# One more pair of output tiles by seven products, rope tables in slots, and an instruction order planned with other TensorE costs, in a hybrid MLA and sparse-attention block

## The chip, the cores and the metric

The kernel runs on one core of a Trainium2 chip. A time is the device time of one execution in microseconds (us). The program drives five engines, each with its own queue of instructions: TensorE (PE, with its weight loads shown apart as PEld), VectorE (DVE), ScalarE (ACT), GpSimd (POOL) and SyncE (SP), which issues most of the loads and stores. All values are 32-bit floats.

## What is computed

One pre-norm layer on x, 512 tokens by 1024 channels, with two token mixers that read one combined projection of the normalised input. Cut to what matters:

```python
h = rmsnorm(x, norm_g)
(q_lat, c_kv, k_rope, z_a, q_b, k_b, v_b, z_b,
 q_idx, k_idx, w_idx, gate_a, gate_b) = split(h @ w_in)
q  = rmsnorm(q_lat) @ w_uq          # 8 heads, 64 plain and 32 rotary channels
kv = rmsnorm(c_kv) @ w_ukv          # 8 heads, 64 key and 64 value channels
y_a = chunk_causal_attention(q, kv, rope(k_rope)) * silu(z_a)        # branch a, MLA
score = sum_h w_idx * relu(q_idx . k_idx)     # masked by chunks of 64
idx = top_k(score, 128)                       # per query
y_b = attention(q_b, k_b[idx], v_b[idx], t5_bias) * silu(z_b)        # branch b, DSA
merged = sigmoid(gate_a) * (y_a @ w_o_a) + sigmoid(gate_b) * (y_b @ w_o_b)
out = rmsnorm(x + merged @ w_out, final_g)
```

The gathered attention of branch b is computed as dense attention with a mask of the selected keys.

## The kernel before

**Tiles and products.** Work lies in tiles of 128 partitions by 512 columns. On-chip memory is a pool of 73 such slots (`SB`), four buffers for raw weights of 128 by 1024 (`RAW`), some fixed tiles, and eight PSUM banks. A product of full precision is made of three products of rounded parts: each operand is split into a high part (a cast, on ACT, L381) and a low part (the value less the high part, on DVE, L416, or on POOL, L418), and `mm3` multiplies high by high, high by low and low by high (L494). `split_w` and `split_t` make the parts of a weight, and `act` and `tt` record an operation on ACT, DVE or POOL. L513 is the transposes (`turn`), L523 the DMAs on SP.

A *single* tile (`proj`, a lower-case name in the queue) is 128 output channels by 512 tokens: 8 steps over the channels of h, three matmuls of 512 columns each, 24 in all, and two splits of weights. A *pair* (`proj2`, two upper-case names) makes two such tiles at once, split in halves of tokens and channels, by seven products instead of eight (`seven`): 84 matmuls of 256 columns in place of 48 of 512. In return it needs sums of raw weights (`prep`, in the raw tiles and in `wsum` slots), sums of the input's halves (`input_sums`, `hs`, made once), seven splits instead of four, and it is put together in two `pair` slots by copies on ACT and two 256-wide adds on DVE.

**Stages.** First the latents of both branches from x (`early_x`, `early_w`, `early_mm`; 0 to some 60 us); then the projections, in the order of a list `QUEUE` (ga and gb the gates, za and zb the SiLU inputs, ma and va the MLA queries, keys and values, sb and VB the DSA queries, keys and values, pe the rotary part), with other work between them: the index scores (L961), the top-k rounds on DVE (16 rounds of MAX8, L986, and MATCH_REPLACE8, L987, for each of three masks), eight MLA heads and eight DSA heads. In the profile an MLA head is three matmuls of logits (L1909 to L1911), maxima on DVE (TENSOR_REDUCE, L1893), exponentials on ACT, transposes, high and low parts of the transposed probabilities (`ph`, `last`) and the product with the values (`vv`). A DSA head has its softmax in one custom operation on DVE (L1992). Then come the products with w_o, the seven products with w_out, and the final norm with the stores of the result.

**What sets the order.** `Flow` is a planner in the kernel's Python: each operation is a `Step` with a cost and the engines that can take it; threads with priorities yield steps, ask for slots (`Get`) or wait for conditions (`Until`), and at each turn the step that could start first by the model's times is emitted. So the place of every instruction in all five queues, and whether DVE or POOL does a subtraction, follows from `QUEUE`, from the priorities and caps below it (`PSCORE` for the index scores, `PHEAD` for the heads, `PHCAP`, `WCAP`, `TCAP`, `PCAP` for how many slots of a kind may be in use), and from the costs: `stream(n)` is that of a matmul of n columns, `turn` that of a transpose.

**Loads on the path.** MLA head logits read q and k tiles that SP's DMAs fill (`s_op`), the last of them with the shared rotary key (`kpeh`, `kpel`, the high and low parts). The same queue of SP takes raw weights (`raw<-w_ga` and so on; `fetcher`, 512 KB for a single tile) and spills of the a-branch's gates to memory (`bias_scratch<-s_sig`, 256 KB).

Of the kernel before, what the change touches and what calls it, by code (L numbers as in the profile page):

```python
# [20 lines left out]
P = 128  # L21
# [18 lines left out]
NSLOT = 73  # L40
# [260 lines left out]
def tile_block(ctx: ExitStack, tc: tile.TileContext, a: dict, out: bass.AP, bias_dram: bass.AP):  # L301
# [13 lines left out]
    def fixed(name, shape, dt=F32):  # L315
        return Buf(const.tile(shape, dt, name=name), name)
# [9 lines left out]
    SB = Pool_([Buf(None, f"s{i}") for i in range(NSLOT)], fresh)  # L326
# [158 lines left out]
    def stream(n):  # L485
        return max(0.0134 + n / 2400, 0.109)
# [20 lines left out]
    def turn(parts):  # L507


        def emit():  # L510
            for d, s in parts:
                product_to(d, True)
                nc.tensor.transpose(d.ap, s.ap, ident.tile)  # L513

        return pe(0.0875 * len(parts), [d for d, _ in parts], [s for _, s in parts] + [ident.all], emit, len(parts))
# [58 lines left out]
    ropec = fixed("ropec", [P, S])  # L574
    ropes = fixed("ropes", [P, S])
# [5 lines left out]
    junk = fixed("junk", [P, S])  # L581
# [5 lines left out]
    rbs = fixed("rbs", [P, P], F32R)  # L587
# [38 lines left out]
    def setup_pool():  # L626
# [6 lines left out]
        yield from pool_dma(ropec.all, a["ropec"])  # L633
        yield from pool_dma(ropes.all, a["ropes"])
# [91 lines left out]
    rbc = []  # L726
# [131 lines left out]

    def rope(dst, src, rows):
# [4 lines left out]
        yield tt(dst, src, ropec[rows], ALU.mult)  # L864
        yield tt(sw.all.f[rows], sw.all.f[rows], ropes[rows], ALU.mult, BOTH)
# [211 lines left out]
    def bias_table():  # L1077
        yield is_done("loads", BIAS_AT)

        yield from pool_dma(rb.all, a["rel_bias"])  # L1080
        yield memset("POOL", rbs.all.f, 0.0)
# [20 lines left out]
        put(*oh, toep, toep2)  # L1102
# [1343 lines left out]
NORM_ABIAS = -0.4  # L2446
# [133 lines left out]
```

## Time and profile before

| | |
|---|---|
| median of 3 runs | 428.67 us (427.9 to 429.76) |
| the profiled execution | 429.5 us, its span 427.7 us |
| mean granted TensorE clock in it | 0.991 |
| PE, DVE, ACT, POOL busy | 97%, 88%, 69%, 24% of the span |
| moved by DMA | 65.91 MB, mean 154 GB/s |

The span runs from the first to the last instruction in the trace; the 1.8 us between span and time lie around it. Busy times of neighbours that overlap in an engine's pipeline are counted once in the windows of the trace, while a group's mean is that of a single instruction from its own start to its own end, so counts times means come out above the busy time of a window.

### The profile page before, as it was taken

Reading aid. Unit: us, or ns where it says so; the run is one execution under the profiler, and the core shown is the slowest. Engines: PE = TensorE matmul, PEld = TensorE weight load, DVE = VectorE, ACT = ScalarE, POOL = GpSimd, SP = SyncE. Lnnn points to the kernel's source line nnn. Section 1 sums busy time; section 2 is a strip of 40 time slices with the busy share of each in tenths; the row PEclk is TensorE's granted clock in tenths of the full one; section 3 lists DMA queues with packets and bytes.
Section 4 is the critical chain, followed back from the end, with each engine's and each line's share of the span. In section 5 each row is a group of like instructions: output and inputs, shape, how many; then the busy total and the mean of one; then the engine's idle time right before and its main releaser. Section 6 shows DMA issues by size and latency. Waiting matters only on the chain.

```text
span 427.7 us, 7455 instructions
## 1 busy us (share of the span) xinstructions
PE 415.5 (97%) x2451; PEld 369.4 (86%) x2451; DVE 375.5 (88%) x801; ACT 293.5 (69%) x669; POOL 101.6 (24%) x126
## 2 busy tenths in 40 slices
PE   8999999899999999999999999999999999999993
PEld 6989888698888888888999998999988888888882
DVE  4869779589999999998969959999989876999994
ACT  5876986368685847648857698898689643348534
POOL 1032856122854442811112002111000000000212
PEclk9999999989999999999999999999999999999998
DMA  8982645605645361350243644522583884458105
GB/s 260 396 311 69 163 116 154 179 2 129 193 123 159 99 203 49 94 166 25 100 149 111 183 140 103 157 64 85 164 267 125 263 280 171 172 163 329 50 1 197
DMA packets 30279, 65.91 MB, mean 154 GB/s; under 512 B 4648, under 2 KB 5688, under 8 KB 30240
## 3 DMA queue, kind: packets, MB, share of 16 engines
q1 hardware_dynamic: 29120, 63.82, 47.2%
q0 software_dynamic: 832, 1.22, 1.0%
q8 instruction: 19, 0.31, 0.3%
q10 hardware_dynamic: 288, 0.39, 0.3%
q14 instruction: 20, 0.16, 0.1%
HBM read 50.49 MB, written 4.21 MB: 128 GB/s over the span
## 4 chain that ended last, share of the span: by engine, by line
PE 63%; DVE 17%; DMA 9%; ACT 5%; issue 3%; SPq 2%; POOL 0%; POOLq 0%; ACTq 0%; DVEq 0%
PE ps L494 54%; PE ps L513 5%; DVE s_w L416 2%; DVE s_wo L416 2%; DMA raw<-w_o 2%; DVE s_mg L416 2%; ACT s_w L381 2%; SPq L523 2%; DMA s_op<-kpel 1%; DMA raw<-w_ql 1%; DMA s_x<-xT 1%; DMA s_xn<-x 1%; DVE s_pair L416 1%; DVE s_rg L416 1%; PE ps L1910 1%
## 5 line engine op out<-in xcount | busy, mean ns | idle before, releaser
L494 PE MATMUL ps<-s_h,s_w 128*128 128x512 f32 (+1 forms) x684 | 149.5, 357 | 1.1 <-ACT s_pair L381 0.6
L494 PEld LDWEIGHTS ps<-s_h,s_w 128*128 128x128 f32 x684 | 110.3, 189 | 15.6 <-ACT s_pair L381 1.5
L381 ACT CAST s_w<-raw 128x512 fp32r<-128x512 f32 (+3 forms) x132 | 76.0, 595 | 22.0 <-DMA raw<-w_o 12.7
L416 DVE TENSOR_TENSOR s_w<-raw,s_w 128x512 fp32r<-128x512 f32 (+2 forms) x95 | 62.1, 674 | 3.9 <-ACT s_w L381 3.5
L418 POOL TENSOR_TENSOR s_w<-raw,s_w 128x512 fp32r<-128x512 f32 (+2 forms) x37 | 44.5, 1207 | 61.7 <-ACT s_w L381 30.7
L494 PE MATMUL ps<-s_hs,s_w 128*128 128x256 f32 x336 | 46.7, 285 | 0.0
L494 PE MATMUL ps<-s_ys,s_w 128*128 128x512 f32 x192 | 43.9, 389 | 0.0
L494 PEld LDWEIGHTS ps<-s_hs,s_w 128*128 128x128 f32 x336 | 42.8, 191 | 0.4 <-DVE s_w L416 0.2
L494 PEld LDWEIGHTS ps<-s_ys,s_w 128*128 128x128 f32 x192 | 36.0, 188 | 7.4
L494 PE MATMUL ps<-s_w,s_xg 128*128 128x328 f32 (+1 forms) x192 | 33.1, 325 | 0.3 <-ACT s_rbc L381 0.2
L494 PE MATMUL ps<-s_wo,s_mg 128*128 128x512 f32 (+1 forms) x156 | 33.0, 373 | 0.0
L494 PEld LDWEIGHTS ps<-s_w,s_xg 128*128 128x128 f32 x192 | 31.3, 188 | 1.2 <-ACT s_rbc L381 0.5
L494 PEld LDWEIGHTS ps<-s_wo,s_mg 128*128 128x128 f32 x156 | 27.6, 188 | 5.2
L390 ACT ACTIVATE s_p<-ps,sm 128x128 f32<-128x128 f32 (+3 forms) x32 | 16.9, 528 | 17.7 <-DVE sm L1893 17.5
L390 ACT ACTIVATE s_p<-s_p,sm 128x512 f32<-128x512 f32 (+3 forms) x52 | 28.7, 571 | 0.1
L986 DVE MAX8 sm<-mask 128x8 f32<-128x256 f32 (+2 forms) x48 | 25.6, 550 | 0.6 <-POOL mask L568 0.2
L987 DVE MATCH_REPLACE8 mask<-sm,mask 128x256 f32<-128x256 f32 (+2 forms) x48 | 26.0, 543 | 0.1
L513 PE MATMUL ps<-ident,s_p 128*128 128x128 f32 x160 | 23.1, 274 | 0.0
L494 PE MATMUL ps<-s_lat,s_w 128*128 128x512 f32 x78 | 20.7, 397 | 0.0
L513 PEld LDWEIGHTS ps<-ident,s_p 128*128 128x128 f32 x160 | 18.5, 140 | 2.1
L1992 DVE CUSTOM_DVE_ANT_0 s_p<-ps,mask 128x128 f32<-128x128 f32 (+3 forms) x32 | 15.1, 488 | 5.7 <-PE ps L494 5.3
L418 POOL TENSOR_TENSOR s_pair<-s_pair 128x256 f32<-128x256 f32 x1 | 0.7, 743 | 81.2 <-issue 81.2
(213 smaller groups left out, 800.2 us busy)
## 6 DMA issues: line engine op xcount, KB each, us to landing
raw<-w_out SPq DMA_DIRECT2D x18, 512.0 KB, 4.6
s_op<-s_op SPq DMA_DIRECT2D x36, 128.0 KB, 2.7
raw<-w_ga SPq DMA_DIRECT2D x8, 512.0 KB, 4.3
raw<-w_gb SPq DMA_DIRECT2D x8, 512.0 KB, 4.3
raw<-w_o SPq DMA_DIRECT2D x16, 256.0 KB, 3.1
s_x<-xT SPq DMA_DIRECT2D x8, 256.0 KB, 4.0
s_xn<-x SPq DMA_DIRECT2D x8, 256.0 KB, 5.7
raw<-w_za SPq DMA_DIRECT2D x4, 512.0 KB, 4.8
```

Of the source, the lines that this page charges most:

```text
L381: nc.scalar.copy(dst.ap, src.ap)
L390: nc.scalar.activation(dst.ap, src.ap, func, **kw)
L416: opts.append(("DVE", 0.07 + 0.00104 * x.n + few(x), lambda: nc.vector.tensor_tensor(dst.ap, x.ap, y.ap, op=op)))
L418: opts.append(("POOL", 0.15 + 0.0021 * x.n, lambda: nc.gpsimd.tensor_tensor(dst.ap, x.ap, y.ap, op=op)))
L494: nc.tensor.matmul(ps.ap, l.ap, r.ap, start=start and i == 0, stop=stop and i == len(pairs) - 1, skip_group_check=more)
L513: nc.tensor.transpose(d.ap, s.ap, ident.tile)
L523: return Step([("SP", n / 360000.0, lambda: nc.sync.dma_start(d, s))], bufs(dst), bufs(src))
L986: yield Step([("DVE", t, lambda: nc.vector.max(m8.tile, work.ap))], [m8], [mask[i]])
L987: yield Step([("DVE", t - 0.009, lambda: nc.vector.match_replace(work.ap, m8.tile, work.ap, MARK))], [mask[i]], [m8])
L1910: nc.tensor.matmul(o, q0[0:96], k1[0:96], start=False, stop=False)
L1992: step = Step([("DVE", 0.1 + 0.00104 * n, lambda: nc.vector.tensor_tensor_reduce(p.ap, ps.tile[:, :n], mask[i].tile, op0=ALU.add, op1=ALU. ...
```

## The change

1. **Costs of the order's model.** `stream(n)` from 0.0134 + n/2400 to 0.0148 + n/2400 (0.0133 + n/2400 at 256 columns), a transpose in `turn` from 0.0875 to 0.109 us.
2. **Slots.** The rope tables move from fixed tiles into slots that come free after their three users; `rbs` (the bias table's weights) and `rbc` (the row of norms) are given back after use; `junk` becomes bfloat16; 78 slots instead of 73. Raw tiles of at most 512 columns (sixteen of w_o, two of w_va) go to slots of a class `ro`, at most four at once (`ROCAP`), instead of `RAW`.
3. **Queue.** zb0, ga6, ga7 and zb3 were single and ZB1, ZB2 a pair; now GA6, GA7 are a pair, ZB0, ZB1 another and ZB2, ZB3 a third, and VB stands ahead of GA6.
4. **Priorities and caps**, among them the index scores from 10 to 3 (a lower number goes first among threads that could start at the same time), the heads from 4 to 8.

```diff
-NSLOT = 73
+NSLOT = 78
...
-        return max(0.0134 + n / 2400, 0.109)
+        return max(0.0148 + n / 2400, 0.109) - 0.0015 * (n == 256)
...
-        return pe(0.0875 * len(parts), [d for d, _ in parts], [s for _, s in parts] + [ident.all], emit, len(parts))
+        return pe(0.109 * len(parts), [d for d, _ in parts], [s for _, s in parts] + [ident.all], emit, len(parts))
...
-    ropec = fixed("ropec", [P, S])
-    ropes = fixed("ropes", [P, S])
...
-    junk = fixed("junk", [P, S])
+    junk = fixed("junk", [P, S], BF16)
...
-    rbs = fixed("rbs", [P, P], F32R)
...
-        yield from pool_dma(ropec.all, a["ropec"])
-        yield from pool_dma(ropes.all, a["ropes"])
+        for name in ("ropec", "ropes"):
+            t = yield slot("rope")
+            yield from pool_dma(t.all.f, a[name])
+            turns.append(t)
...
+    def rbc_done():
+        rbc_users[0] -= 1
+        if not rbc_users[0]:
+            put(rbc[0])
...
+        rbs = yield slot("oh")
         yield from pool_dma(rb.all, a["rel_bias"])
-        yield memset("POOL", rbs.all.f, 0.0)
+        yield memset("POOL", rbs[:, :P].f, 0.0)
...
-            raw = yield Get(RAW)
+            raw = (yield slot("ro", ROCAP)) if sum(job.widths) <= S and ROCAP else (yield Get(RAW))
...
-NORM_ABIAS = -0.4
+NORM_ABIAS = 0.0
...
-PHCAP = 5
-WCAP = 12
-TCAP = 5
+PHCAP = 7
+WCAP = 10
+TCAP = 7
...
-PSCORE = 10.0
+PSCORE = 3.0
 PFILL = 12.0
-PHEAD = 4.0
-OUT_AT = (2, 3, 5, 10, 10, 10, 14)
+PHEAD = 8.0
+OUT_AT = (2, 3, 5, 9, 10, 11, 13)
 ORDER = [0,1,2,3]
-QUEUE = 'ga0 ga1 pe ma0 ga2 za0 va1 va0 ma1 ga3 za1 ma2 ga4 ga5 ma3 za2 za3 sb0 zb0 ga6 ga7 VB SB1 GB0 GB1 SB2 ZB1 ZB2 GB2 GB3 SB3 GB4 GB5 zb3 gb6 ou ou gb7 ou'
-LATE = 0.4
+QUEUE = 'ga0 ga1 pe ma0 ga2 za0 va1 va0 ma1 ga3 za1 ma2 ga4 ga5 ma3 za2 za3 sb0 VB GA6 GA7 SB1 GB0 GB1 SB2 ZB0 ZB1 GB2 GB3 SB3 GB4 GB5 ZB2 ZB3 gb6 ou ou gb7 ou'
+LATE = 0.75
...
-SPARE = {'w': 3, 'wo': 6, 'sig': 3}
+SPARE = {'w': 2, 'wo': 6, 'sig': 3}
 XOUT = 0
-PSUMS = 8.0
-PCAP = 11
+PSUMS = 5.0
+PCAP = 14
 BIAS_AT = ('a', 1)
 NHELD = 3
-SUMS_AT = ('a', 6)
+ROCAP = 4
+SUMS_AT = ('a', 5)
```

Counted in the order, matmuls of `s_h` with `s_w` of 512 columns go from 432 to 336, those of 256 columns (with `s_h` or `s_hs`) from 588 to 756; DVE has 783 instructions instead of 752, POOL 119 instead of 131, ACT 601 instead of 585, SP 246 instead of 245.

**SP around the first loads of the rotary key.** `s_op` are the key tiles of the first two MLA heads, `raw` the weight buffers, `bias_scratch` the spill. Before:

```order
L523 DMA raw_68<-w_uqkv 128x640
L523 DMA s_op_984<-kpeh 36x512
L523 DMA raw_69<-w_ga 128x1024
L523 DMA bias_scratch<-s_sig_1053 128x512
L523 DMA s_op_986<-kpel 32x512
L523 DMA s_op_1024<-kpeh 36x512
L523 DMA s_op_1026<-kpel 32x512
```

And after the change:

```order
L523 DMA s_op_982<-kpeh 36x512
L523 DMA bias_scratch<-s_sig_1058 128x512
L523 DMA s_op_984<-kpel 32x512
L523 DMA s_op_1025<-kpeh 36x512
L523 DMA s_op_1027<-kpel 32x512
L523 DMA raw_67<-w_ga 128x1024
L523 DMA raw_68<-w_ga 128x1024
```

The load of w_ga has moved from ahead of the first `kpel` to behind both; the spill stays ahead of it.

**DVE around the first maximum of MLA.** `mask` holds the scores of one block of queries, `sm` small results, `s_z` a SiLU tile. Before:

```order
L428 SCALAR_TENSOR_TENSOR mask_112<-ps_99,widx,mask_112 128x512
L428 SCALAR_TENSOR_TENSOR mask_110<-ps_99,widx,mask_110 128x256
L986 MAX sm_83<-mask_110 128x8
L987 MATCH_REPLACE mask_110<-sm_83,mask_110 128x256
L986 MAX sm_84<-mask_110 128x8
L987 MATCH_REPLACE mask_110<-sm_84,mask_110 128x256
L986 MAX sm_85<-mask_110 128x8
L428 SCALAR_TENSOR_TENSOR s_z_1108<-s_z_1108,ps_95 128x512
L1893 TENSOR_REDUCE sm_86<-ps_98 128x1
```

And after the change:

```order
L999 MATCH_REPLACE mask_108<-sm_82,mask_108 128x256
L998 MAX sm_86<-mask_109 128x8
L998 MAX sm_85<-mask_108 128x8
L999 MATCH_REPLACE mask_109<-sm_86,mask_109 128x384
L428 SCALAR_TENSOR_TENSOR mask_110<-ps_98,widx,mask_110 128x512
L999 MATCH_REPLACE mask_108<-sm_85,mask_108 128x256
L998 MAX sm_87<-mask_109 128x8
L998 MAX sm_88<-mask_108 128x8
L1906 TENSOR_REDUCE sm_89<-ps_99 128x1
```

Two masks' top-k rounds have begun ahead of the first maximum where there was one; that maximum is the 133rd instruction of DVE instead of the 126th.

**DVE up to the low part of DSA head 1's transposed probabilities** (`s_ph` of 384 columns, the last row of each). `s_wsum` and `raw<-raw` are sums of weights for pairs, `s_w` low parts of weights, `s_pair` a pair being put together, L2005 the softmax. Before:

```order
L416 TENSOR_TENSOR vv_70<-s_pair_2423,vv_70 128x2x4x64
L416 TENSOR_TENSOR s_wsum_2787<-raw_66 128x512
L416 TENSOR_TENSOR raw_66<-raw_66,raw_67 128x512
L416 TENSOR_TENSOR s_w_2748<-raw_69,s_w_2738 128x512
L416 TENSOR_TENSOR s_y_2804<-ps_95,s_tmp_2796 64x512
L416 TENSOR_TENSOR s_ph_2784<-ps_97,s_ph_2446 128x512
L416 TENSOR_TENSOR s_ph_2791<-ps_96,s_ph_2785 128x384
```

And after the change:

```order
L416 TENSOR_TENSOR s_pair_2953<-ps_92,s_pair_2951 128x256
L416 TENSOR_TENSOR raw_68<-raw_68 128x512
L416 TENSOR_TENSOR s_w_3150<-s_wsum_3039,s_w_3148 128x512
L416 TENSOR_TENSOR s_ph_3024<-ps_96,s_ph_3023 128x512
L416 TENSOR_TENSOR s_w_3185<-raw_68,s_w_3184 128x512
L416 TENSOR_TENSOR s_w_3202<-raw_67,s_w_3201 128x512
L416 TENSOR_TENSOR s_pair_2953<-ps_92,s_pair_2953 128x256
L416 TENSOR_TENSOR s_op_3214<-s_pair_2951,s_op_3213 128x512
L416 TENSOR_TENSOR s_ph_3090<-ps_97,s_ph_3025 128x384
```

That low part is the 462nd instruction of DVE instead of the 402nd, and work for a pair (adds into `s_pair`, low parts from `s_wsum`) stands ahead of it where the values' evictions (`vv`) stood.

More of the change, by code (lines that the diff above doesn't have):

```diff
@@ L324, in fresh @@
         return slots.tile([P, S], F32R if cls in rounded else F32, tag=b.name, name=f"{b.name}_{cls}{uid[0]}", bufs=1)
-    SB = Pool_([Buf(None, f"s{i}") for i in range(NSLOT)], fresh)
+    SB = Pool_([Buf(None, f"s{i}") for i in range(NSLOT + 8 - 2 * NRAW)], fresh)
     RAW = Pool_([fixed(f"raw{i}", [P, 1024]) for i in range(NRAW)])
@@ L724, in x_squares @@
         done.add("x loads")
-    rbc = []
+    rbc, rbc_users = [], [NK + 2]
+    def rbc_done():
+        rbc_users[0] -= 1
+        if not rbc_users[0]:
+            put(rbc[0])
     def split_w(raw, w, dst, key, cls="w", cap=None, release=False, early=False, added=False, high=None):
@@ L835, in normed @@
         yield stt(x.all.f, x.all.f, normg[:, k : k + 1], rbc[0].all.f, ALU.mult, ALU.mult)
+        rbc_done()
         hi = yield slot("h")
@@ L857, in square_sum @@
         return step
+    turns, turn_users = [], [3]
     def rope(dst, src, rows):
@@ L863, in rope @@
                    [sw], bufs(src))
-        yield tt(dst, src, ropec[rows], ALU.mult)
-        yield tt(sw.all.f[rows], sw.all.f[rows], ropes[rows], ALU.mult, BOTH)
+        c, sn = turns
+        yield tt(dst, src, c.all.f[rows], ALU.mult)
+        yield tt(sw.all.f[rows], sw.all.f[rows], sn.all.f[rows], ALU.mult, BOTH)
+        turn_users[0] -= 1
+        if not turn_users[0]:
+            put(c, sn)
         yield tt(dst, dst, sw.all.f[rows], ALU.add)
@@ L910, in take_qi @@
             yield tt(tmp.all.f[:, SCORED], banks[m][:, SCORED], rbc[0].all.f[:, SCORED], ALU.mult)
+            rbc_done()
             put(banks[m])
@@ L1096, in bias_table @@
             yield pe(0.148, [ps.all], [rbs.all, o.all], lambda: (product_to(ps[:, :320], True), nc.tensor.matmul(
-                ps.tile[:, :320], rbs.tile, o.tile[:, :320], start=True, stop=True)))
+                ps.tile[:, :320], rbs.tile[:, :P], o.tile[:, :320], start=True, stop=True)))
             yield act(tp.all.f[:NH, : c1 - c0], ps[:NH, : c1 - c0] if BADD else backward(ps[:NH, : c1 - c0]))
@@ L1101, in bias_table @@
             yield from pool_dma_out(bass.AP(bias_dram.tensor, c0 if BADD else NREL - c1, [[NREL, NH], [1, c1 - c0]]), tp.all.f[:NH, : c1 - c0])
-        put(*oh, toep, toep2)
+        put(rbs, *oh, toep, toep2)
         done.add("bias")
```

## The prediction

> **What bounds the kernel now.** I read the page first (busy shares, chain of waits), then the table of windows, then the timeline at the few places where TensorE (PE) stops, then the groups by line for the prices.
>
> ```profile
> span 427.7 us, 7455 instructions
> PE 415.5 (97%) x2451; PEld 369.4 (86%) x2451; DVE 375.5 (88%) x801; ACT 293.5 (69%) x669; POOL 101.6 (24%) x126
> ...
> PE 63%; DVE 17%; DMA 9%; ACT 5%; issue 3%; SPq 2%; POOL 0%; POOLq 0%; ACTq 0%; DVEq 0%
> ```
>
> PE is busy 97% of the span, so at first sight PE alone sets the time, and fewer PE microseconds are a shorter kernel. But VectorE (DVE) is at 88%, and that is a mean. The windows (start:end, length, then PE, PEld, DVE, ACT, POOL busy with counts, clock, DMA share, GB/s) show where it is full:
>
> ```profile
> 0.00:73.00 73.00, 71.18 (x387) 63.19 (x388) 56.86 (x114) 56.24 (x126) 29.03 (x43) 1.00 0.63 208
> 85.50:98.00 12.50, 12.50 (x78) 11.80 (x78) 10.71 (x34) 8.45 (x24) 3.37 (x5) 0.86 0.01 2
> 98.00:211.00 113.00, 112.93 (x617) 97.03 (x616) 110.38 (x264) 79.92 (x190) 47.54 (x57) 1.00 0.44 127
> 211.00:231.20 20.20, 20.20 (x169) 20.11 (x168) 16.82 (x28) 13.78 (x27) 2.59 (x2) 1.00 0.26 85
> 231.20:320.00 88.80, 87.63 (x678) 84.11 (x676) 79.65 (x168) 73.52 (x177) 9.10 (x7) 1.00 0.51 152
> 371.00:411.00 40.00, 40.00 (x190) 33.55 (x189) 39.93 (x74) 20.29 (x40) 3.34 (x3) 1.00 0.45 158
> 0.00:85.50 85.50, 81.84 (x439) 72.13 (x440) 64.13 (x130) 60.07 (x134) 32.17 (x47) 1.00 0.64 206
> 85.50:231.20 145.70, 145.63 (x859) 128.94 (x859) 137.91 (x324) 102.15 (x240) 53.50 (x64) 0.99 0.37 110
> ```
>
> Between 98 and 211 us DVE is busy 110.38 of 113.00 and PE 112.93: the two are bound together, DVE by the top-k rounds, the softmax maxima and the low parts of split weights. Only in 211 to 320 (3.4 and 9.2 us idle) has DVE room. So there are two clocks to follow: PE's work, and DVE's work from the first MLA maximum (the first TENSOR_REDUCE) to the low part of DSA head 1's transposed probabilities, which PE then reads. I call that the stretch; the windows put it at 85.5 to 231.2. The one real hole in PE lies just ahead of it (start, duration, instruction):
>
> ```profile
> 77.89 0.40 SPq L523 DMA_DIRECT2D raw<-w_ga  x1
> 78.35 0.42 SPq L523 DMA_DIRECT2D bias_scratch<-s_sig  x1
> 78.82 0.58 SPq L523 DMA_DIRECT2D s_op<-kpel  x1
> ...
> 82.94 0.22 PE L1909 MATMUL ps<-s_op,qhi 100*128 100x128 f32 x1
> ...
> 85.00 0.33 PE L1910 MATMUL ps<-s_op,qhi 96*128 96x128 f32 x1 [1.84 <-DMA s_op<-kpel]
> ...
> 85.48 0.29 DVE L1893 TENSOR_REDUCE sm<-ps 128x1 f32<-128x128 f32 x1 [1.69 <-PE ps L1911]
> ```
>
> A small load (kpel) sits in SP's queue behind a 512 KB weight load and a 256 KB spill; PE waits 1.84 us for it, and the granted clock is 0.86 in the 12.5 us behind (0.14 x 12.5 = 1.75 us more).
>
> **The change, step by step.**
>
> *Pairs on PE.* Four single tiles become two pairs: 96 matmuls of 512 columns go, 168 of 256 come. Price of each, from unbroken runs (start, length, count):
>
> ```profile
> 339.79 12.41 PE L494 MATMUL ps<-s_ys,s_w 128*128 128x512 f32 x54
> ...
> 205.61 2.39 PE L494 MATMUL ps<-s_w,s_hs 128*128 128x256 f32 x18
> ...
> 208.09 3.12 PE L494 MATMUL ps<-s_w,s_hs 128*128 128x256 f32 x24
> ...
> 211.04 2.20 PE L494 MATMUL ps<-s_w,s_h 128*128 128x256 f32 x17
> ```
>
> Take off a last matmul of 0.39 (512) or 0.28 (256) and divide by the steps: (12.41 - 0.39)/53 = 0.227 us; (2.39 - 0.28)/17 = 0.124, (3.12 - 0.28)/23 = 0.123, (2.20 - 0.28)/16 = 0.120. I take 0.227 and 0.120: 96 x 0.227 - 168 x 0.120 = 21.8 - 20.2 = 1.6 us less PE work; with 0.124 it is 1.0. [...]
>
> *What the pairs and the new order cost DVE.* A pair needs four sums of raw weights, seven low parts instead of four, and two adds when it is evicted: per pair 7 more 512-wide operations and 2 of 256. Beside that 12 low parts go from POOL to DVE (POOL falls from 131 to 119 instructions, DVE rises from 752 to 783 in the order). Prices (count, busy, mean ns):
>
> ```profile
> L416 DVE TENSOR_TENSOR s_w<-raw,s_w 128x512 fp32r<-128x512 f32 x20 | 14.0, 720 | 1.9 <-ACT s_w L381 1.8
> L416 DVE TENSOR_TENSOR s_ph<-ps,s_ph 128x512 fp32r<-128x512 f32 x10 | 6.8, 684 | 0.1
> L416 DVE TENSOR_TENSOR s_pair<-ps,s_pair 128x256 f32<-128x256 f32 x14 | 5.9, 419 | 0.5 <-PE ps L494 0.4
> L418 POOL TENSOR_TENSOR s_w<-raw,s_w 128x512 fp32r<-128x512 f32 x21 | 27.2, 1298 | 44.1 <-ACT s_w L381 26.7 <-ACT s_ph L381 13.4 <-DVE s_hs L416 1.5
> ```
>
> Over the kernel that is 26 x 0.685 + 4 x 0.42 = 19.5 us at full price. PE has 97% and no room, DVE has 52 us idle, so over the whole kernel it would fit. But the pair of ga6 and ga7 stands where single tiles stood, and the new priorities put DSA head 1 later against the queue of tiles, so that two and a half pairs more are multiplied ahead of it. Most of the added DVE work, and some that came later, lands in the stretch: counted there in the order, 512-wide adds and subtracts go from 58 to 105, 256-wide from 9 to 19, and five of the top-k's and one of the values' fall out of it (3.4 us): 47 x 0.70 + 10 x 0.42 - 3.4 = 33.7 us (0.70 between the rows' 0.720 and 0.684). Neighbours overlap on DVE: the 276 operations of before sum to 155.9 us at their means, while the window shows 137.91 busy, a factor 0.885. So the stretch's DVE work grows from 137.9 by 33.7 x 0.885 = 29.8 to 167.7 us.
>
> *PE's work in the same stretch* (from the first MLA logit to the matmul that reads that low part): 512-wide 359 to 289, 256-wide 320 to 612, the rest the same within three: -70 x 0.227 + 292 x 0.120 = +19.1, with those three +19.5: 142.4 to 161.9 us. Before, PE's 142.4 exceeded DVE's 137.9 by 4.5; after, DVE's 167.7 exceeds PE's 161.9 by 5.8. This is the turn of the whole case: **in this stretch DVE becomes the bound**.
>
> *POOL beside DVE.* The low parts on DVE take 720 ns beside POOL's and 684 where POOL is quiet: 20 x 0.036 = 0.7 us, which shrinks when POOL does less. [...] I leave the 0.7 as a gain inside the range.
>
> *kpel.* In the new SP order only a 256 KB spill stands right ahead of kpel; the two 512 KB loads nearest to it are issued earlier or behind it. The wait and the slow clock (1.84 + 1.75 = 3.6 us) should go. They are worth that to PE alone; DVE gets at most what its own start allows, next.
>
> *DVE's start.* Up to the first maximum the order has 132 DVE operations where there were 125, 75.1 us against 71.3 at full price, so 3.8 x 0.885 = 3.4 more than the 64.1 busy by 85.5 us (56.86 by 73, the rest behind it). Idle was 73.00 - 56.86 = 16.1 up to 73, and 5.2 from there to 85.5, where the index scores came late and the kpel hole followed. Scores come first now (priority 3 instead of 10). With the 16.1 kept and the 5.2 gone, DVE reaches its first maximum at 64.1 + 3.4 + 16.1 = 83.6; PE has that logit at about 82.6 (its work up to there is 1.0 less). So DVE starts the stretch at 83.6 instead of 85.5.
>
> *The end.* From the low part on, PE work is 182.2 before (432 x 0.227 + 598 x 0.120 + the small ones) and 162.0 after (408 and 480). Before it takes:
>
> ```profile
> 230.11 1.14 DVE L416 TENSOR_TENSOR s_ph<-ps,s_ph 128x512 fp32r<-128x512 f32 x2
> ...
> 232.56 0.98 PE L494 MATMUL ps<-s_ph,vv 128*128 128x512 f32 x4
> ...
> 416.68 3.70 PE L494 MATMUL ps<-s_wo,qhi 128*128 128x512 f32 x27
> ```
>
> The low part is done at 231.25 and PE reads it in that group at about 233.0; its last matmul ends at 420.4: 187.4 us, so 5.2 of small waits on top of 182.2. The tail after it is 427.7 - 420.4 = 7.3. DVE work from there on falls by 14 us against PE's 20.
>
> *The rest.* Rope tables, rbs and rbc in slots, and five more slots, change addresses and when tiles come free, not the work: 0 while loads are early; the same 16 w_o loads are issued, from other buffers. ACT waits 12.7 us for them in all (below), but PE is busy all of 345 to 371 us, so they are covered there; with that cover gone they would be worth up to 12.7. A bfloat16 junk changes only what ACT writes and nobody reads: 0.1 either way.
>
> ```profile
> L381 ACT CAST s_w<-raw 128x512 fp32r<-128x512 f32 (+3 forms) x132 | 76.0, 595 | 22.0 <-DMA raw<-w_o 12.7
> ```
>
> **The sum.** 83.6 (DVE's first maximum) + 167.7 (its work) + 1.0 idle + 0.3 (hand-over) = 252.6 for PE's read; + 162.0 + 5.2 + 7.3 = 427.1 us of span, against 427.7. Around the span lie 429.5 - 427.7 = 1.8, so 428.9 for a run like the profiled one; that run is 0.8 above the median of 428.67, so **428.0 us** to the half microsecond that this sum is good for. The gains on PE (1.6 and 3.6) are real and are nearly all taken back by DVE. The 1.0 idle is the weakest number: below, it is 0 (427.0); above, 7.8, what the window of before shows in all (145.70 - 137.91).
>
> **Rivals.**
>
> A, *PE keeps the pace* (faster). DVE's added operations overlap more, or the idle of 16.1 at the start is partly used, so that DVE never holds PE up. Then PE's own sum: first logit 81.9 + 161.9 + 4.0 of small waits (150.1 us before from 82.94 to 233.0, less 142.4 and less 3.6) + 162.0 + 5.2 + 7.3 = 422.3, so 423.3 us against the median. For it: the page's 97%, and that DVE at 110.38 of 113.00 is slowed by a PE that is itself full. Against: 5.8 us have to be found in a stretch that is full already. Anything between, from 0.85 instead of 0.885 as overlap, gives 423 to 426.
>
> B, *DVE idles in the DSA heads of the stretch or behind it* (slower). Place: from the end of the top-k rounds, where each DSA softmax waits for logits on PE and each low part for a cast on ACT. These waits stood in before's slack:
>
> ```profile
> DVE s_w L416 <- ACT s_w L381: 5.7, 10, 1.0
> DVE s_p L1992 <- PE ps L494: 5.3, 9, 1.1
> ```
>
> Before, they were free, since PE had more to do than DVE. In a stretch bound by DVE each such wait is a delay. Price: 3.4 of idle as in 211 to 231, plus 2.6 as in 98 to 211, in place of my 1.0: +5.0, 433.0 us. It turns to slower from 3.8 us of idle in the stretch (428.0 + 2.8 = 430.8). The second place is behind the stretch: there DVE's spare time shrinks by 20 - 14 = 6 us of the 9.2 that it had to 320.
>
> C, *the pairs save nothing*: at 0.130 (3.12/24, the run of the row above with its last matmul left in) a pair is 84 x 0.130 = 10.9 us against 48 x 0.227 = 10.9. Then PE's rest grows by half of 1.6, 0.8, and the time is 428.8: level.
>
> **How the numbers follow.** A measurement of this kernel can tell about 0.5%, 2.1 us, from no change: level is 426.5 to 430.8. Forecast 0.40 (of it 0.26 level, 0.08 faster, 0.06 slower, since its one free number has more room above than below but DVE's start may also come earlier), A 0.30, B 0.20, C 0.10. So faster 0.30 + 0.08 = 0.38; level 0.26 + 0.10 = 0.36; slower 0.20 + 0.06 = 0.26. Cases of both signs hold most of the chance; the forecast's own range is 426 to 431. The range reaches to A's 423.3 below and most of the way to B's 433.0 above: 423.3 to 432.5.
>
> **What would show it.** Right: no wait of PE for kpel and a clock of 1.00 in 85 to 98; first TENSOR_REDUCE near 83.6; DVE busy over 98% from there to the low part of DSA head 1, and that low part at about 252; PE showing small waits on DVE there; DVE busy about 394 us in all, POOL about 84. Wrong: DVE idle over 4 us in the stretch, or the low part before 249 (A), PE waiting for DMA at another place, a pair of matmuls at 0.13 each, or DVE's busy sum well under 390.

## The result and the profile after

The changed kernel takes 422.69 us (median of 4 runs, 422.53 to 423.33) against 428.28 us (427.28 to 429.76) for the kernel before: a ratio of 0.987 [0.984, 0.990], 5.6 us faster. The forecast was 428.0, with a range from 423.3; rival A had 423.3. The page of the changed kernel (line numbers from L961 on are 12 to 14 higher than before; those of the helpers, L381 to L523, are the same):

```profile
span 420.8 us, 7599 instructions
PE 412.4 (98%) x2523; PEld 370.1 (88%) x2523; DVE 389.4 (93%) x832; ACT 297.1 (71%) x684; POOL 83.7 (20%) x114
...
PE 82%; issue 7%; DVE 7%; ACT 2%; POOL 1%; POOLq 0%; DVEq 0%
```

VectorE is busier (389.4 for 375.5 us), POOL less (83.7 for 101.6), as the count of instructions said. But the chain that ended last has gone over to TensorE: 82% of it, where it was 63%, and VectorE's share fell from 17% to 7%. The windows (columns as in the prediction; the last row is the stretch):

```profile
73.00:98.00 25.00, 24.97 (x147) 21.89 (x146) 24.64 (x65) 17.53 (x44) 9.78 (x16) 1.00 0.35 103
98.00:211.00 113.00, 112.99 (x689) 100.15 (x688) 112.04 (x254) 71.72 (x166) 37.72 (x48) 1.00 0.40 118
231.20:320.00 88.80, 88.80 (x698) 86.70 (x697) 81.39 (x187) 79.54 (x197) 3.88 (x3) 1.00 0.45 131
83.00:249.00 166.00, 165.81 (x1092) 150.93 (x1090) 163.65 (x376) 117.88 (x280) 43.53 (x57) 1.00 0.42 123
```

Both engines are full: in the stretch TensorE 165.81 and VectorE 163.65 of 166.00. (Busy is not the same as working at the usual step: from the first logit at 82.2 to the read at 249.8 TensorE took 167.6 us, where the steps at their usual length sum to 161.9, and yet all but 0.19 of the stretch shows as busy. The steps are counted below.) Between 231.2 and 320, where TensorE had lost 1.2 us before, it now loses nothing that the windows show. The few rows that carry the prediction's steps, from the timeline:

```profile
78.39 0.40 SPq L523 DMA_DIRECT2D bias_scratch<-s_sig  x1
78.91 0.57 SPq L523 DMA_DIRECT2D s_op<-kpel  x1
...
81.00 0.53 SPq L523 DMA_DIRECT2D raw<-w_ga  x1
...
82.25 0.27 PE L1923 MATMUL ps<-s_op,qhi 96*128 96x128 f32 x1
...
82.97 0.28 DVE L1906 TENSOR_REDUCE sm<-ps 128x1 f32<-128x128 f32 x1
...
248.48 0.55 DVE L416 TENSOR_TENSOR s_ph<-ps,s_ph 128x384 fp32r<-128x384 f32 x1
...
249.35 0.98 PE L494 MATMUL ps<-s_ph,vv 128*128 128x512 f32 x4
```

And the waits of TensorE, all that its list has (waits over 0.15 us; total, times, longest):

```profile
PE ps L618 <- DVE neghalf L568: 1.0, 1, 1.0
PE ps L513 <- POOL rstd L468: 0.4, 1, 0.4
```

The kpel hole is gone (the logit's second matmul follows the first within 0.06 us), and the list has no wait of TensorE on VectorE, on ACT or on a load after the start.

Where the 6.9 us between the two spans went, worked out from the starts of neighbouring matmuls. Each step up to the next matmul is compared with the usual one of its width (0.227 at 512 columns, 0.120 at 256, 0.174 at 384 and so on); these are the median steps in both kernels. The matmuls' own work, all at the usual step, is 405.8 before and 404.2 after: -1.6. The steps beyond it are 13.3 and 8.8: -4.5, of which -3.2 lie at 80 to 100 us (the kpel hole), -2.6 at 240 to 320 us (3.2 to 0.6), and +1.2 elsewhere. The tail behind the last matmul goes from 7.3 to 6.5: -0.8. The profiled run of before (429.5) was 1.2 above its median, that of after (422.5) 0.2 below its own, so some 1.4 of the 6.9 is a difference of runs.

### The profile page after: what moved, and what is told of

It is laid out like the page before. It is cut to its first block, busy times and chain, and to the rows that moved or that the text cites. A ratio compares the mean times of both kernels' runs of the same rounds, so it can differ in the third digit from the quotient of the medians.

```text
span 420.8 us, 7599 instructions
## 1 busy us (share of the span) xinstructions
PE 412.4 (98%) x2523; PEld 370.1 (88%) x2523; DVE 389.4 (93%) x832; ACT 297.1 (71%) x684; POOL 83.7 (20%) x114
## 4 chain that ended last, share of the span: by engine, by line
PE 82%; issue 7%; DVE 7%; ACT 2%; POOL 1%; POOLq 0%; DVEq 0%
PE ps L494 72%; PE ps L513 5%; DVE s_w L416 3%; PE ps L1922 1%; PE ps L1923 1%; DVE raw L416 1%; PE ps L1924 1%; ACT s_w L381 1%; PE ps L973 1%; DVE mask L999 1%; DVE sm L998 1%; DVE vv L416 0%; DVE s_wsum L416 0%; DVE s_y L416 0%; POOL rstd L468 0%
## 5 line engine op out<-in xcount | busy, mean ns | idle before, releaser
L494 PE MATMUL ps<-s_h,s_w 128*128 128x512 f32 (+1 forms) x660 | 132.5, 342 | 0.1
L494 PEld LDWEIGHTS ps<-s_h,s_w 128*128 128x128 f32 x660 | 102.5, 189 | 11.4 <-ACT s_pair L381 0.4
L381 ACT CAST s_w<-raw 128x512 fp32r<-128x512 f32 (+2 forms) x118 | 68.6, 595 | 10.2 <-DVE raw L416 8.9
L416 DVE TENSOR_TENSOR s_w<-raw,s_w 128x512 fp32r<-128x512 f32 (+2 forms) x92 | 58.9, 662 | 5.0 <-ACT s_w L381 4.6
L494 PE MATMUL ps<-s_hs,s_w 128*128 128x256 f32 x432 | 59.8, 285 | 0.0
L494 PEld LDWEIGHTS ps<-s_hs,s_w 128*128 128x128 f32 x432 | 55.2, 191 | 0.5 <-ACT ps L381 0.2
L418 POOL TENSOR_TENSOR s_w<-raw,s_w 128x512 fp32r<-128x512 f32 (+2 forms) x26 | 29.9, 1155 | 64.5 <-PE ps L494 33.9
L416 DVE TENSOR_TENSOR s_ph<-ps,s_ph 128x512 fp32r<-128x512 f32 (+1 forms) x32 | 19.1, 620 | 1.1 <-ACT s_ph L381 1.1
L381 ACT COPY s_pair<-ps 128x256 f32<-128x256 f32 (+1 forms) x40 | 15.6, 390 | 5.8 <-PE ps L494 5.7
```

What stands on the lines that cost most here:

```text
L381: nc.scalar.copy(dst.ap, src.ap)
L416: opts.append(("DVE", 0.07 + 0.00104 * x.n + few(x), lambda: nc.vector.tensor_tensor(dst.ap, x.ap, y.ap, op=op)))
L418: opts.append(("POOL", 0.15 + 0.0021 * x.n, lambda: nc.gpsimd.tensor_tensor(dst.ap, x.ap, y.ap, op=op)))
L494: nc.tensor.matmul(ps.ap, l.ap, r.ap, start=start and i == 0, stop=stop and i == len(pairs) - 1, skip_group_check=more)
```

## The experiments

Ratios are to the kernel before, timed beside each run; its medians there were 427.9 to 428.4 us. "Slower than changed" is against the 422.7 of the result, which was timed apart from them, so that a few tenths of such a difference mean nothing. Sums of steps beyond the usual in a window are from the profiled run, and with another choice of the usual step they move by some 0.2 us. In e1, e2, e5, e6 and e7 all queues keep their order, so nothing is planned anew; in the others the planner sets the order again.

**e1: the kernel before, kpel ahead of the w_ga load and the spill.**

```diff
-        return Step([("SP", n / 360000.0, lambda: nc.sync.dma_start(d, s))], bufs(dst), bufs(src))
+        def go():
+            number[0] += 1
+            if number[0] in (71, 72):
+                behind_it.append(lambda: nc.sync.dma_start(d, s))
+                return None
+            made = nc.sync.dma_start(d, s)
+            if number[0] == 75:
+                for issue in behind_it:
+                    issue()
+            return made
+
+        return Step([("SP", n / 360000.0, go)], bufs(dst), bufs(src))
```

> The kernel before with every queue in its old order, save that the 512 KB load of w_ga and the 256 KB spill that stood ahead of the first two kpel loads in SP's queue are issued behind them. Theory P (the time is TensorE's own work plus its holes, and VectorE nowhere holds it up for long): the hole of 1.84 us and the slow clock behind it (1.75 us) go, and nothing takes their place: 3.0 to 3.6 us faster than before, near 425. Theory D (the prediction's: VectorE sets the pace from the first maximum on): VectorE is at 110.38 of 113 us there and has top-k rounds to do while TensorE waits, so the gain is eaten: under 1 us.

Measured: 426.83 us (425.81 to 428.11), ratio 0.997 [0.996, 0.999]: 1.3 us faster. No wait for kpel is left, and the clock is 1.00 from 73 to 98. The median lies between the theories, nearer to D's figure. The two profiled runs have P's: their spans are 3.7 us apart (427.7 and 424.0), and 3.4 of that lies at 80 to 100 us. So the hole was paid in full there, and VectorE did not take the gain back; but the profiled run of before, with a mean granted clock of 0.991, isn't the usual one. Of the 76 runs of before timed beside all experiments, 14 had a mean clock of 0.993 or less and took 429.8 us in the median; the other 62 took 427.9. The hole was worth less in the median than in the profiled run of before.

**e2: the changed kernel, kpel behind the w_ga load** (the same edit with numbers 72 and 74 held until 75).

> The changed kernel with its order kept, save that its first two kpel loads are issued behind the w_ga load that follows them, as they stood before. Theory P: a hole of TensorE of 1.5 to 2 us and a slow clock behind it come back, 2 to 3.5 us slower than the changed kernel (424.7 to 426.2). Theory D: VectorE works through top-k rounds meanwhile and sets the pace later, so under 1 us is lost.

Measured: 426.30 us (424.65 to 426.92), ratio 0.994 [0.992, 0.996]: 3.6 slower than changed. The longest wait that came in, in TensorE's waits:

```profile
PE ps L1936 <- DMA s_op<-kpel: 1.9, 1, 1.9
```

P's side, a little above its range. The slow clock did not come back: it is 1.00 in 85.5 to 98. Of the 3.5 us between this profiled run and that of the changed kernel, 1.9 is the hole, 0.5 lies ahead of the first logit, 0.4 behind the low part and 0.7 in the tail. So the hole is paid in full; the rest isn't traced to it.

**e3: the pairs undone in the changed kernel** (`QUEUE` of before, all else new).

> The changed kernel with the old queue: zb0, ga6, ga7, zb3 single again, ZB1 and ZB2 a pair; costs, slots and priorities stay new (the order is planned anew behind the first heads; VectorE has 757 instructions instead of 783, POOL 126 instead of 119). Theory P: TensorE's work is 1.1 to 1.6 us more and the holes stay closed: 423.8 to 424.5. Theory D: VectorE has 26 instructions, some 16 us, less, which where it sets the pace makes the kernel faster than the changed one: 419 to 421.5.

Measured: 428.29 us (427.26 to 430.37), ratio 1.000 [0.998, 1.002]: 5.6 slower than changed, the whole gain. Neither theory has that: P allowed for 1.8 at most, D for a gain. In its trace TensorE's work at the usual step is 1.6 us more, and waits came back that the changed kernel doesn't have, at the first DSA heads and at the splits:

```profile
PE ps L494 <- DMA qhi<-s_op: 0.7, 1, 0.7
PE ps L494 <- ACT s_w L381: 0.5, 1, 0.5
```

Between the two profiled runs (4.8 us apart) 1.7 of the steps beyond the usual lie at 180 to 200 us, where the first DSA heads are, and 1.2 at 240 to 320.

**e4: the pairs alone in the kernel before** (`QUEUE` of after, all else old).

> The kernel before with nothing but the new queue (the pairs; VectorE 778 instructions instead of 752); the w_ga load and the spill still stand ahead of kpel. Theory P: 1.1 to 1.6 us faster than before, the hole at 83 us stays: 426.5 to 427.2. Theory D: VectorE's added work lands where it is full: slower than before by 1 to 4 us.

Measured: 442.29 us (442.10 to 443.53), ratio 1.033 [1.030, 1.036]: 14 us slower than before. The sign is D's, the size is nobody's. VectorE is no fuller there than before (busy 109.17 of the 113.00 us from 98 to 211, for 110.38); the timeline of TensorE shows a hole instead:

```profile
184.71 1.57 PE L494 MATMUL ps<-s_w,s_hs 128*128 128x256 f32 x11 [1.95 <-DVE s_w L416]
...
187.52 1.22 PE L494 MATMUL ps<-s_w,s_hs 128*128 128x256 f32 x4 [0.26 <-DVE s_hs L416]
192.12 0.80 PE L494 MATMUL ps<-s_w,s_hs 128*128 128x256 f32 x2 [3.38 <-ACT s_hs L381]
```

TensorE waits for `s_hs`, the sums of the input's halves that every pair multiplies. In this kernel they are cast between 174 and 192 us:

```profile
L381 ACT CAST s_hs<-s_x x6: 614/621/626, 174.3 to 186.5; 128x512 fp32r<-128x512 f32 x6
L381 ACT CAST s_hs<-s_tmp x2: 620/620/621, 191.4 to 192.1; 128x512 fp32r<-128x512 f32 x2
```

In the changed kernel between 154 and 170:

```profile
L381 ACT CAST s_hs<-s_x x6: 607/614/622, 154.2 to 164.4; 128x512 fp32r<-128x512 f32 x6
L381 ACT CAST s_hs<-s_tmp x2: 619/621/623, 169.3 to 170.3; 128x512 fp32r<-128x512 f32 x2
```

The steps beyond the usual sum to 10.2 us between 180 and 200; in the changed kernel to nothing. Not all of it is waiting: the granted clock is 0.74 in these 20 us, and 1.00 in the changed kernel, so that, by an estimate, some 5 us (0.26 x 20) of the 10.2 are matmuls at the slower clock.

**e5: 4.8 us more work for VectorE in the changed kernel.**

```diff
-            yield Step([("DVE", 0.07 + 0.00104 * n, lambda: nc.vector.tensor_reduce(
-                mx.tile[:, 1:2], ps.tile[:, :n], op=ALU.max, axis=AX.X, negate=True))], [mx], [ps])
+            def biggest():
+                for _ in range(2 if n == S else 1):
+                    made = nc.vector.tensor_reduce(mx.tile[:, 1:2], ps.tile[:, :n], op=ALU.max, axis=AX.X, negate=True)
+                return made
+
+            yield Step([("DVE", 0.07 + 0.00104 * n, biggest)], [mx], [ps])
```

> The changed kernel in its own order, with the 512-wide maximum of each MLA head taken twice on VectorE: 8 operations, 8 x 0.60 = 4.8 us more VectorE work between 83 and 172 us, the same result. Theory P: the work fits behind TensorE's: under 1 us slower than the changed kernel (below 423.7). Theory D: VectorE sets the pace there, so 3 to 4.8 us slower (425.7 to 427.5).

Measured: 429.01 us (428.54 to 429.79), ratio 1.003 [1.001, 1.004]: 6.3 slower than changed. D's side, and more than D. VectorE has 5.6 us more busy time (395.0), 0.70 for each of the eight. TensorE's waits show how it arrives:

```profile
PE ps L513 <- DVE s_ph L416: 1.0, 3, 0.4
...
PE ps L513 <- POOL s_p L450: 0.6, 2, 0.3
PE ps L1926 <- ACT s_p L390: 0.5, 2, 0.3
```

Each is a link of a head's chain (maximum, exponential, scaling, transpose, low part) that comes late.

**e6: 3.3 us more work for TensorE in the changed kernel.**

```diff
+                if nn > 2 * P:
+                    nc.tensor.matmul(o, q0[0:100], k0[0:100], start=True, stop=True)
                 nc.tensor.matmul(o, q0[0:100], k0[0:100], start=True, stop=False)
```

> The changed kernel in its own order, with the first of the three logit matmuls of 384 and 512 columns issued twice in every MLA head: 16 matmuls, 8 x 0.235 + 8 x 0.176 = 3.3 us more TensorE work, the same result. Theory P: 3.0 to 3.5 us slower (425.7 to 426.2). Theory D: hidden behind VectorE: under 1 us.

Measured: 425.45 us (425.22 to 425.87), ratio 0.994 [0.993, 0.996]: 2.8 slower than changed. P: most of it is paid. Had VectorE set the pace by several microseconds, as the prediction had it, it would have been hidden.

**e7: 5.1 us less work for VectorE in the changed kernel.**

```diff
-            yield Step([("DVE", t, lambda: nc.vector.max(m8.tile, work.ap))], [m8], [mask[i]])
-            yield Step([("DVE", t - 0.009, lambda: nc.vector.match_replace(work.ap, m8.tile, work.ap, MARK))], [mask[i]], [m8])
+            kept = i < NT - 1 or r < TOPK // 8 - 4
+            yield Step([("DVE", t, lambda: kept and nc.vector.max(m8.tile, work.ap))], [m8], [mask[i]])
+            yield Step([("DVE", t - 0.009, lambda: kept and nc.vector.match_replace(work.ap, m8.tile, work.ap, MARK))], [mask[i]], [m8])
```

> The changed kernel in its own order, with the last 4 of the 16 top-k rounds of the 512-wide mask left out (fewer keys are selected for the last block of queries): 4 x (0.60 + 0.60 + 0.08) = 5.1 us less VectorE work ahead of the DSA heads. Theory P: at most 0.5 us faster than the changed kernel (422.2 or above). Theory D: 2 to 4 us faster (418.7 to 420.7).

Measured: 422.83 us (422.76 to 423.63), ratio 0.989 [0.987, 0.990]: as the changed kernel. P. (It leaves out four rounds, so it selects fewer keys.) In the changed kernel these rounds lie at 192 to 203 us. The part of the stretch from which they are taken, in the windows of this kernel and then of the changed one:

```profile
173.00:249.00 76.00, 75.97 (x609) 74.54 (x608) 70.36 (x138) 59.66 (x134) 7.26 (x8) 1.00 0.45 130
```

```profile
173.00:249.00 76.00, 75.85 (x610) 74.39 (x608) 74.20 (x150) 59.46 (x135) 6.57 (x7) 1.00 0.45 133
```

VectorE now idles 5.6 us of 76, for 1.8 there, and TensorE goes on as before.

Since e5, e6 and e7 keep the order of the changed kernel, their traces can be laid beside its own, place by place (us; the read is TensorE's first matmul on the low part of DSA head 1, the tail is what follows the last matmul):

| | first logit | read | from logit to read | tail |
|---|---|---|---|---|
| changed | 82.2 | 249.8 | 167.6 | 6.5 |
| e5, VectorE +5.6 | 83.2 | 256.4 | 173.2 | 7.0 |
| e6, TensorE +3.2 | 83.1 | 253.0 | 169.9 | 6.5 |
| e7, VectorE -4.1 | 83.2 | 250.4 | 167.2 | 6.5 |

All three start the stretch 0.9 to 1.0 us later than the changed kernel's profiled run, though nothing differs up to there; 0.6 to 1.1 us more of waiting for POOL's `rstd` stands in their lists. In the stretch itself VectorE's added 5.6 us cost 5.6, TensorE's added 3.2 (16 matmuls at 0.227 and 0.174) cost 2.2, and what was taken from VectorE brought 0.4.

So e5 to e7 together: from 192 us on VectorE has room of some 4 us and TensorE sets the pace. Ahead of that, where e5 and e6 add their work (83 to 173 us), both engines are full (VectorE 89.44 and TensorE 89.96 of 90.00 us in the changed kernel), and added work is paid on VectorE in full (5.6 of 5.6) and on TensorE for the larger part (2.2 of 3.2). No run took work from VectorE there. And the second maximum of e5 stands in each head's chain from logits to exponentials, so that e5 by itself cannot tell a full VectorE from a longer chain.

**e8: pairs alone, with the input sums earlier** (e4 and `SUMS_AT = ('a', 5)`, `PSUMS = 5.0`).

> The kernel before with the new queue and, beside it, the input sums that every pair needs made earlier (after MLA head 5 instead of 6, at priority 5 instead of 8): slots, costs and the other numbers stay old. The pairs alone cost 14 us, and the trace shows TensorE waiting 8 us for the sums near 190 us. Theory P (the waits are the cost; the sums late is one, slots and caps another): the hole near 190 goes and 8 to 12 of the 14 us with it: 430 to 434. Theory D (VectorE's added work is the cost): the sums only move and the work stays, so under 4 us come back: 438 or more.

Measured: 439.86 us (438.79 to 443.92), ratio 1.028 [1.025, 1.030]: 2.4 of the 14 us come back, D's figure. But D's reason isn't seen: the steps beyond the usual at 180 to 200 us fall from 10.2 to 1.4, as P has it, while others grow behind (at 320 to 340 from 3.5 to 6.5), with waits for weights and evictions. The profiled run was the slowest of six (443.9, against 442.1 for that of e4): its kpel hole took 4.1 us more, from a wait of 1.9 for 0.7 and a clock of 0.73 for 1.00 in 85.5 to 98, which says nothing of the sums.

```profile
PE ps L494 <- DVE s_w L416: 2.5, 2, 1.5
PE ps L1910 <- DMA s_op<-kpel: 1.9, 1, 1.9
PE ps L494 <- ACT ps L381: 1.8, 4, 0.8
PE ps L494 <- ACT s_w L381: 1.5, 3, 0.6
```

**e9: slots undone in the changed kernel** (`NSLOT = 73`, `ROCAP = 0`; the rope tables and the other two stay in slots, so that these 73 hold more than those of before).

> The changed kernel with 73 slots instead of 78 and the w_o and w_va tiles in the raw buffers again (rope tables stay in slots). Two theories of why the pairs need the rest of the change. Theory S (room: a pair holds more tiles at once, and the freed slots are what feeds it): 4 us or more slower than the changed kernel. Theory N (numbers: the order's costs, priorities and caps decide, the slots are spare): under 2 us slower.

Measured: 432.46 us (430.39 to 434.49), ratio 1.009 [1.006, 1.012]: 9.8 slower than changed. S. The largest part, some 4.5 us, lies at 400 to 420, where the split weights of the last product come late:

```profile
411.61 0.50 PE L494 MATMUL ps<-s_wo,s_mg 128*128 128x512 f32 x1 [1.87 <-ACT s_wo L381]
412.78 5.54 PE L494 MATMUL ps<-s_wo,s_mg 128*128 128x512 f32 x17 [0.66 <-DVE s_wo L416]
```

**e10: the old costs in the changed kernel** (`stream` and `turn` of before).

> The changed kernel with the old costs of a matmul and a transpose in the order's model; queue, slots, priorities and caps stay new. Theory S: under 2 us slower than the changed kernel. Theory N: 3 us or more slower, with small waits of TensorE spread over the heads, since the planner then places VectorE's work against a TensorE that is faster than the chip's.

Measured: 423.45 us (423.08 to 424.01), ratio 0.988 [0.985, 0.990]: 0.8 slower than changed. S's figure: setting TensorE's costs right is a small part of it.

**e11: the old numbers in the changed kernel** (all priorities and caps of before).

> The changed kernel with the old priorities and caps; queue, slots and costs stay new. Theory S: under 3 us slower than the changed kernel. Theory N: 6 us or more slower, most of it where TensorE waits for the input sums and the weights of the first pair, as with the pairs alone.

Measured: 435.02 us (434.75 to 437.28), ratio 1.016 [1.013, 1.019]: 12.3 slower than changed. N; 6.6 us of it at 180 to 200, where the granted clock is 0.83.

**e12: pairs and slots in the kernel before.**

> The kernel before with the new queue and the new slots (rope tables in slots, 78 slots, w_o in slots); costs, priorities and caps stay old. The pairs alone took 14 us more than before. Theory S: the slots bring back more than half of that: 434 or less. Theory N: less than a third: 438 or more.

Measured: 437.12 us (436.07 to 437.87), ratio 1.019 [1.016, 1.022]: 5.2 of the 14 us come back, between the theories, so neither S nor N alone holds. What is left is almost one place:

```profile
187.43 1.15 PE L494 MATMUL ps<-s_op,qhi 128*128 128x128 f32 x4 [6.20 <-ACT ps L381]
189.41 1.60 PE L494 MATMUL ps<-s_op,qhi 128*128 128x256 f32 x4 [0.83 <-ACT ps L381]
```

ACT copies the bias for these DSA logits behind its casts of the late `s_hs`, which wait 2.69 us for VectorE and 1.35 for POOL, and TensorE waits for the copy. The waits for such copies are 7.9 us in TensorE's list; the granted clock is 0.66 in 180 to 200, and together the steps beyond the usual are 13.8 us there. Of this came theory H: one hole, made by late sums, and slots for what the pairs hold later.

**e13: pairs, slots and early sums in the kernel before** (e12 and the two numbers of e8).

> The kernel before with the new queue, the new slots, and the input sums made earlier (after MLA head 5 at priority 5); costs and all other priorities and caps stay old. Theory H (the price of the new queue is one hole at 180 to 200 us, where the sums are late, and slots for what the pairs hold later on): the hole of 13.6 us of e12 goes and nearly nothing comes in its place: 423 to 427. Theory N (the priorities and caps as a whole): the waits turn up elsewhere, as they did in e8: 432 or more.

Measured: 428.38 us (426.29 to 430.39), ratio 1.001 [0.999, 1.003]: 8.7 less than e12, and level with the kernel before. H's hole is gone (13.8 us to nothing), but 428.4 is between the theories. The profiled run, at 430.4 one of the two slowest of twelve, has new waits at 260 to 280, the longest on a load that stands behind a weight load in SP's queue:

```profile
PE ps L494 <- DMA qhi<-s_op: 2.6, 1, 2.6
...
PE ps L494 <- DVE s_w L416: 0.8, 1, 0.8
```

**e14: the changed kernel with the sums late** (`SUMS_AT = ('a', 6)`, `PSUMS = 8.0`).

> The changed kernel with the input sums made late again (after MLA head 6 at priority 8), all else new. Theory H: a hole of 6 to 14 us at 180 to 200 us comes back: 429 to 436. Theory N: the other numbers cover for it: under 3 us slower than the changed kernel (below 425.7).

Measured: 435.95 us (435.58 to 436.38), ratio 1.019 [1.016, 1.022]: 13.3 slower than changed. H, at its upper end:

```profile
188.19 1.38 PE L494 MATMUL ps<-s_op,qhi 128*128 128x128 f32 x4 [5.72 <-ACT ps L381]
191.40 0.80 PE L494 MATMUL ps<-s_op,qhi 128*128 128x256 f32 x2 [1.84 <-ACT ps L381]
```

The same wait as in e12, with a clock of 0.74: 11.3 us in all at 180 to 200.

**e15: the old caps in the changed kernel.**

```diff
-PHCAP = 7
-WCAP = 10
-TCAP = 7
+PHCAP = 5
+WCAP = 12
+TCAP = 5
...
-SPARE = {'w': 2, 'wo': 6, 'sig': 3}
+SPARE = {'w': 3, 'wo': 6, 'sig': 3}
...
-PCAP = 14
+PCAP = 11
```

> The changed kernel with the old caps on slots (PHCAP 5, WCAP 12, TCAP 5, PCAP 11, SPARE of w 3), all else new. Theory H: under 2 us slower than the changed kernel (below 424.7). Theory N: 3 us or more slower.

Measured: 426.00 us (425.01 to 426.71), ratio 0.995 [0.993, 0.997]: 3.3 slower than changed; N. TensorE waits 2.5 us for low parts of transposed probabilities, whose slots `PHCAP` allots; that the slots are the cause isn't shown.

**e16: the old priorities of scores and heads in the changed kernel** (`PSCORE = 10.0`, `PHEAD = 4.0`).

> The changed kernel with the old priorities of index scores (10) and heads (4), all else new. Theory H: under 2 us slower than the changed kernel, unless a load holds up the first heads again (then the 1.3 us of e1 beside). Theory N: 3 us or more slower.

Measured: 434.77 us (432.69 to 435.71), ratio 1.016 [1.012, 1.019]: 12.1 slower than changed; N. 5.6 us lie at 180 to 200 here too, now as waits for the pairs' weights:

```profile
PE ps L494 <- DVE s_w L416: 4.4, 3, 2.0
PE ps L494 <- ACT s_w L381: 1.5, 1, 1.5
```

## Why the prediction was wrong

**The step that failed** is "in this stretch DVE becomes the bound", by 5.8 us. It was one subtraction of two large sums, and both were off. The sum for VectorE was 4.0 too high: it was busy 163.7 us from its first maximum (82.97) to the end of the low part (248.48 + 0.55 = 249.03), not 167.7. The sum for TensorE, 161.9, has the bare steps alone, without the 4.0 of small waits that rival A's sum adds; from its first logit (82.2) to the read (249.8) TensorE took 167.6 us, 5.7 more than the bare steps, with no wait in its list. So the low part was ready at 249.0 instead of 252.3, and TensorE reached it at 249.8 without waiting: the two engines came out level, and e7 shows that at the end of the stretch it is TensorE that sets the pace. Of the 6.3 us between the forecast span (427.1) and the measured one (420.8) this step is 2.8; the rest lies behind the stretch.

In VectorE's sum two terms were mis-sized. The factor 0.885 was an average over a window with waits in it, applied to added work. In these traces a 512-wide add or subtract that follows another in a full queue starts some 0.08 us before its neighbour ends (the median), and added work also closes gaps: from before to after the overlap in the stretch grew from 18.5 to 25.7 us, 7.2 for the forecast's 3.9. And the operations' own time grew by 33.1 for 33.7, since VectorE got quicker beside a quieter POOL:

```profile
L416 DVE TENSOR_TENSOR s_w<-raw,s_w 128x512 fp32r<-128x512 f32 x44 | 29.0, 687 | 0.5 <-ACT s_w L381 0.3
```

That is 687 ns where it was 720, with POOL busy 43.5 us of the stretch instead of 53.5. The 720 was a mean of two kinds: 18 of the 20 took 684, and the two that ran beside an add or subtract on POOL took 997 and 1092. (The forecast read the 684 of its other row as the same work beside a quiet POOL; that row is another operation, with an input in PSUM, in the same stretch.) Over the whole kernel before, of 225 adds and subtracts of 512 columns on VectorE with both inputs in SBUF (the tiles' memory) 15 ran beside one of POOL and took 905 ns in the mean, the other 210 took 684; with an input in PSUM, 12 ran beside one and took 680, 13 did not and took 687.

**Start of the stretch.** Forecast 83.6, measured 82.97: near, with the idle behind 73 us gone (24.64 busy of 25.00). Two terms behind it were off and cancel in part: VectorE had 68.9 us of work up to there for the forecast's 67.5, and 14.1 of idle for 16.1.

**Idle and hand-over.** Forecast 1.0 and 0.3; measured 166.06 - 163.7 = 2.4, and 0.3 to TensorE's group at 249.35.

**Behind the stretch.** TensorE's work of 162.0 was right, its small waits were not: they were kept at 5.2 and fell to about 2.4 (the read of the low part at some 249.8, the last matmul's end at 414.2). The changed order has no wait of TensorE there at all in the list. Which part of the change closed them was not separated, save that the old costs leave them closed (e10: 164.5 us from the read to the last matmul, as in the changed kernel). The tail is 6.5 for 7.3; it also differs between runs of one order (7.2 in e2, 7.0 in e5), so this 0.8 isn't shown to come from the change. The read came 2.8 us earlier than forecast (249.8 for 252.6); with 2.8 here and 0.8 of the tail that is the 6.3 between 427.1 and 420.8.

**kpel.** The hole went as forecast. Its price of 3.6 was that of one profiled run, with the slow clock in it; e1 puts it at 1.3 in the median, e2 at 3.6 in the order of the changed kernel, of which its trace has 1.9 in the hole.

**The pairs' gain on TensorE** of 1.6 was right: both kernels have median steps of 0.227 and 0.120, and by these the sums differ by 1.6.

**"The rest", costed at nothing.** The sum was worked out on the changed order, in which slots, priorities and caps already have their effect, so this mistake didn't show in it; as a statement on what the slots do it was wrong. Taken out of the changed kernel, the slots cost 9.8 us (e9) and the numbers 12.3 (e11), where the slots were priced as addresses, with loads as their only use. They are worth that only beside the new queue: with the old queue the same slots, costs and numbers gave nothing (e3). The new queue multiplies the input sums from 181 us on, where it was 204, and the numbers are what makes them early; taking these two numbers alone out costs 13.3 us (e14).

**Rival A** had the right figure (423.3 for 422.69) and, at the end of the stretch and behind it, the right mechanism: TensorE keeps the pace. That the figure is so near is in part luck. TensorE reached the read 2.0 us later than A has it (249.8 for 247.8), which the waits behind the stretch (2.8 less) and the tail (0.8 less) more than made up. A's doubt, that 5.8 us would have to be found in a full stretch, was answered by the sizes above. Rival B's point, that waits in a full stretch are paid, holds for work that is added (e5), not for this change. C is out: runs of 256-wide matmuls keep their 0.120 us in the changed kernel.

**What stays open:** whether VectorE or TensorE leads between 83 and 190 us, where no run took work from VectorE; and which waits make up the 5.6 of e3 beyond TensorE's 1.6, since the planner orders everything anew there and the trace shows many small waits rather than one.

## What to carry to other kernels

When two engines are both nearly full over a stretch, the difference of two sums of 160 us cannot say which will lead: give the outcome as two cases of like chance, put the small waits into both sums or into neither, and cost added work at the margin (start to start in a full queue), not by the mean over a window with waits. A change of order by a planner is a package: the part that saves work (here 1.6 us) may cost 14 us alone and 5.6 us by its absence, so ask of each tile that is used earlier who makes it, when, and in which slot. Price a stall from several runs, not from the one that was profiled, and look whether the granted clock fell behind it.

## What the runs showed of the hardware

The small load behind a 512 KB load and a spill is not late by a fixed amount: in the profiled run of before kpel landed 6.1 us after its issue and TensorE waited 1.8 us for it; with the same loads ahead of it the wait was 0.7 us in e4, and in e1, without them, TensorE's list has none. Runs of before spread over 426.5 to 430.6 us, and taking that queueing away moved the median by 1.3 us though the profiled run showed 3.6 (1.84 of wait, and an estimated 1.75 of slower clock). The changed kernel, with no wait for a load in TensorE's list, spreads over 0.8 us in its four runs.

The granted clock behind a hole of TensorE was not the same each time: behind the 1.8 us of before it was 0.86 over 12.5 us, behind the 1.9 us of e2 it was 1.00. Behind the longer holes near 187 us it was 0.74 (e4, e14) and 0.66 (e12) over 180 to 200.

In the profiled run of before a 512-wide add or subtract on VectorE with both inputs in SBUF took 684 ns in the mean (210 of them), and 905 where it ran beside one on POOL (15); with an input in PSUM it took 680 beside one (12) and 687 otherwise (13).

And adding 5.6 us of busy time to a full engine, in the chain of each head, made the stretch 5.6 us longer (167.6 to 173.2), while taking 4.1 us of busy time (389.4 to 385.3) from the same engine later on brought 0.4 us there and nothing in the median.
